# Differential attention by heads instead of by token tiles, with paired score matmuls and the output projection in a written order at the end of its layer

## The chip, the cores and the metric

The kernel runs on one core of a Trainium2 chip. The metric is device time in microseconds (us) of one execution; a profile of one execution, taken by the hardware profiler, stands beside it. The engines are TensorE (PE in the profile, with its weight loads as PEld), VectorE (DVE), ScalarE (ACT), GpSimd (POOL) and SyncE (SP), which issues most of the DMAs.

## The reference, cut to what matters

The program is a two-layer decoder trunk over 512 tokens of width 1024, in float32. Layer 0 runs eight heads of latent attention (MLA) and four heads of differential attention side by side, concatenates their outputs and multiplies them by one matrix; a gated ConvFFN follows. Layer 1 (dilated and stick-breaking attention, then another ConvFFN) is not changed. The part in question:

```python
def diff_attention(q1, q2, k1, k2, v, lam, slopes):          # 4 heads, d = 64, v is 128 wide
    def probs(qb, kf):
        s = einsum('bhqd,bhkd->bhqk', qb, kf) * 64 ** -0.5 - slopes * dist
        return softmax(where(causal, s, -inf))
    p = probs(a1, k1) - lam * probs(a2, k2)
    return einsum('bhqk,bhkd->bhqd', p, v)

o_diff = rms_norm(o_diff, subln_g) * (1.0 - lam_init)        # over the 128 columns of a head
out = concatenate([heads_last(o_mla), heads_last(o_diff)]) @ w_out    # 1024 x 1024
x = x + rms_norm(out, post_g)                                 # sandwich norm, then the FFN's pre-norm
```

## The kernel before, in words

Tokens are handled in four tiles of 128 (NT = 4), taken in the order 3, 2, 1, 0 (`ORDER`), so that the tile with the longest causal row comes first. Activations that feed a projection are kept transposed (columns of the model on the 128 partitions, tokens along the free axis), as two parts, a high and a low one (`xh`, `xl`); so are the weights (`wh` by a ScalarE copy on L71, `wl` by a VectorE subtraction on L72). Each product is three matmuls (`mm3`, L259 to L261). `Weights` streams the matrices in the order of `units`: SP issues a 512 KB load into one of three `wraw` buffers, ScalarE and VectorE split it, and TensorE uses it.

The body of `even` (layer 0) writes, in this order:

- the shared input projections, and `diff_qk(0, z)` for head 0: query (z = 0, into `dq`) and key (z = 1, into `dk`) of a head, 24 matmuls of 512 columns each. The 128 rows of `dq[h]` hold the head's two queries, 64 rows each, and `dk[h]` its two keys;
- MLA: 32 units (head, token tile), each with score, transpose and value steps, staggered by `skewed`. Ten fillers stand behind them in the list: `diff_qk` for heads 1 to 3 (six) and `diff_v` for four token tiles (four, 24 matmuls each). The framework's scheduler places filler instructions where TensorE would wait;
- differential attention: 16 units, token tile by token tile, four heads within a tile. A unit makes two score matmuls, on rows 0 to 63 and 64 to 127 (L787), each into one of the two PSUM banks with the tag "s"; after each, VectorE adds the ALiBi table and takes the minimum on L567, ScalarE exponentiates, and VectorE joins the two on L794. `turn` transposes the difference, `value` multiplies by `dv` (L807), scales, squares on ScalarE, takes the root on GpSimd (`rstd`) and scales by `subg` (L813). After the fourth head of a tile `finish` transposes the tile's four outputs (L821) and splits them into `odh` and `odl`;
- the output projection, `project(i)`, for a token tile: two halves of 512 columns with eight terms of three matmuls each, 48 matmuls. It is the last stage of the last unit of the following tile (`after`), so three of the four tiles run among the units of differential attention, and the last one behind all of them. `chain` then makes the residual, the two norms and the transposed input of the FFN.

The scheduler fixes the order of all engines in layer 0. At the end of layer 1 the order of TensorE, VectorE, ScalarE and GpSimd is written out by hand (`manual_schedule`). The FFN of layer 0 begins with token tiles 3 and 2 and takes the pending transposes of the attention layer among its first matmuls (`pending`).

## Time and profile before

| | |
|---|---|
| median of 3 runs | 1173.12 us (1171.82 to 1174.36) |
| the profiled execution | 1173.26 us, span 1171.4 us |
| TensorE busy in the span | 1151.1 us (98%), weight loads 941.4 us (80%) |
| VectorE, ScalarE, GpSimd busy | 811.3 us, 556.9 us, 56.4 us |
| granted TensorE clock | 0.996 |
| first MLA score / last | 64.0 us / 114.1 us |
| first differential score / last | 159.9 us / 214.8 us |
| first matmul of the FFN (`u`) | 248.7 us |

The span runs from the first to the last instruction. Matmuls are pipelined and their ends are modelled: a matmul of 512 columns in the split form is shown as 0.39 us long, while in a dense run one starts every 0.227 us. So the distance from start to start tells the cost, and the idle time in front of an instruction tells a wait. A float32 matmul that is not a transpose appears as two records. The transposes and score matmuls are in float32; the projections are in the split form.

### The profile page before, as it was taken

Reading aid. Unit: us, or ns where it says so; the run is one execution under the profiler, and the core shown is the slowest. Engines: PE = TensorE matmul, PEld = TensorE weight load, DVE = VectorE, ACT = ScalarE, POOL = GpSimd, SP = SyncE. Lnnn points to the kernel's source line nnn. Section 1 sums busy time; section 2 is a strip of 40 time slices with the busy share of each in tenths; the row PEclk is TensorE's granted clock in tenths of the full one; section 3 lists DMA queues with packets and bytes.
Section 4 is the critical chain, followed back from the end, with each engine's and each line's share of the span. In section 5 each row is a group of like instructions: output and inputs, shape, how many; then the busy total and the mean of one; then the engine's idle time right before and its main releaser. Section 6 shows DMA issues by size and latency. Waiting matters only on the chain. (4 is left out here: it accounts for less than half of the span.)

```text
span 1171.4 us, 15164 instructions
## 1 busy us (share of the span) xinstructions
PE 1151.1 (98%) x5656; PEld 941.4 (80%) x5656; DVE 811.3 (69%) x1424; ACT 556.9 (48%) x942; POOL 56.4 (5%) x138
## 2 busy tenths in 40 slices
PE   8999999999999999999999999999999999999997
PEld 7876766788888888888878877897988888888885
DVE  6677358657666666898973465676676766779896
ACT  5565246445343443456553454544444344345562
POOL 2100002310000000000030000002000000000001
PEclk9999999999999999999999999999999999999999
DMA  7320340033323323345725212222233332324461
GB/s 282 113 81 19 115 126 1 37 129 110 106 90 102 97 90 96 100 146 171 236 100 166 88 55 90 91 74 73 95 124 90 95 103 90 105 84 138 146 202 72
DMA packets 39049, 126.81 MB, mean 108 GB/s; under 512 B 4672, under 2 KB 6336, under 8 KB 38848
## 3 DMA queue, kind: packets, MB, share of 16 engines
q1 hardware_dynamic: 37056, 122.11, 32.6%
q10 hardware_dynamic: 1920, 3.74, 1.0%
q8 instruction: 44, 0.72, 0.3%
q14 instruction: 29, 0.24, 0.1%
HBM read 117.95 MB, written 6.29 MB: 106 GB/s over the span
## 5 line engine op out<-in xcount | busy, mean ns | idle before, releaser
L72 DVE TENSOR_TENSOR wl<-wraw,wh 128x1024 fp32r<-128x1024 f32 (+1 forms) x203 | 245.9, 1219 | 185.4 <-ACT wh L71 184.8
L71 ACT CAST wh<-wraw 128x1024 fp32r<-128x1024 f32 (+1 forms) x203 | 210.6, 1046 | 289.7 <-PE u L260 177.9
L260 PE MATMUL u<-xl,wh 128*128 128x512 f32 (+1 forms) x768 | 285.5, 372 | 0.1
L259 PE MATMUL u<-xh,wh 128*128 128x512 f32 (+1 forms) x768 | 285.1, 372 | 0.2 <-ACT xh L170 0.2
L261 PE MATMUL u<-xh,wl 128*128 128x512 f32 (+1 forms) x768 | 285.3, 372 | 0.0
L261 PEld LDWEIGHTS u<-xh,wl 128*128 128x128 f32 x768 | 144.7, 188 | 25.2
L259 PEld LDWEIGHTS u<-xh,wh 128*128 128x128 f32 x768 | 144.5, 188 | 25.4 <-ACT xh L170 0.6
L260 PEld LDWEIGHTS u<-xl,wh 128*128 128x128 f32 x768 | 144.7, 188 | 25.1 <-DVE xl L171 0.3
L261 PE MATMUL acc<-wh,gl 128*128 128x512 f32 x248 | 96.6, 389 | 0.0
L260 PE MATMUL acc<-wl,gh 128*128 128x512 f32 x248 | 96.6, 389 | 0.0
L259 PE MATMUL acc<-wh,gh 128*128 128x512 f32 x248 | 96.5, 390 | 0.0
L408 ACT ACTIVATE y<-u,cw 128x512 f32<-128x512 f32 x88 | 67.4, 773 | 1.8 <-PE u L261 1.8
L413 ACT ACTIVATE y<-y 128x512 f32<-128x512 f32 x44 | 27.7, 632 | 85.1 <-DVE y L411 85.1
L411 DVE SCALAR_TENSOR_TENSOR y<-u,cw,y 128x510 f32<-128x510 f32 x88 | 65.6, 747 | 2.5
L409 DVE SCALAR_TENSOR_TENSOR y<-u,cw,y 128x511 f32<-128x511 f32 x88 | 65.1, 744 | 0.9 <-ACT y L408 0.9
L177 POOL TENSOR_TENSOR rv<-ms,epst 128x1 f32<-128x1 f32 x40 | 11.2, 282 | 913.2 <-ACT junk L229 842.5
L259 PEld LDWEIGHTS acc<-wh,gh 128*128 128x128 f32 x248 | 46.6, 188 | 10.1 <-issue 0.5
L261 PEld LDWEIGHTS acc<-wh,gl 128*128 128x128 f32 x248 | 46.6, 188 | 9.7
L260 PEld LDWEIGHTS acc<-wl,gh 128*128 128x128 f32 x248 | 46.6, 188 | 9.6
L259 PE MATMUL apt<-xh,wh 128*128 128x512 f32 x128 | 50.7, 396 | 0.0
L260 PE MATMUL apt<-xl,wh 128*128 128x512 f32 x128 | 50.0, 391 | 0.0
L261 PE MATMUL apt<-xh,wl 128*128 128x512 f32 x128 | 49.9, 390 | 0.0
(289 smaller groups left out, 1914.5 us busy)
## 6 DMA issues: line engine op xcount, KB each, us to landing
wraw<-in_ffn_w_up SPq DMA_DIRECT2D x88, 512.0 KB, 3.6
wraw<-in_ffn_w_down SPq DMA_DIRECT2D x44, 512.0 KB, 3.7
wraw<-in_od_w_dqk SPq DMA_DIRECT2D x12, 512.0 KB, 3.7
wraw<-in_ffn_w_down SPq DMA_DIRECT2D x22, 256.0 KB, 2.7
wraw<-in_ev_w_dqk SPq DMA_DIRECT2D x8, 512.0 KB, 3.9
wraw<-in_ev_w_out SPq DMA_DIRECT2D x8, 512.0 KB, 3.8
spill<-X SPq DMA_DIRECT2D x8, 512.0 KB, 2.6
X<-spill SPq DMA_DIRECT2D x8, 512.0 KB, 6.5
```

What stands on the lines that cost most here:

```text
L71: self.nc.scalar.copy(h[:, :w], raw[:, :w])
L72: self.nc.vector.tensor_tensor(l[:, :w], raw[:, :w], h[:, :w].bitcast(F32), ALU.subtract)
L177: POOL.tensor_tensor(v[:, :n], ms, epst[:, :n], ALU.add)
L259: PE.matmul(o, lh, rh, start=first, stop=False, skip_group_check=more)
L260: PE.matmul(o, lh, rl, start=False, stop=False, skip_group_check=more)
L261: PE.matmul(o, ll, rh, start=False, stop=last, skip_group_check=more)
L408: ACT.activation(y[:, z], u, AF.Identity, bias=c[:, 3:4], scale=c[:, 2:3])
L409: DVE.scalar_tensor_tensor(y[:, z, 1:], u[:, :S - 1], c[:, 1:2], y[:, z, 1:], ALU.mult, ALU.add)
L411: DVE.scalar_tensor_tensor(y[:, z, 2:], u[:, :S - 2], c[:, 0:1], y[:, z, 2:], ALU.mult, ALU.add)
L413: ACT.activation(y[:, 0], y[:, 0], AF.Silu)
```

## The change

Only layer 0 is changed.

- The weights of `diff_v` are streamed before those of `diff_qk` for heads 1 to 3, and MLA keeps only the four `diff_v` as fillers.
- Differential attention runs head by head, four token tiles within a head. Its fillers, one every two steps, are `diff_qk` for heads 1 to 3, and then the MLA half (four of the eight terms) of the output projection for token tiles 3 and 2, two halves each.
- A unit takes both PSUM banks before its two score matmuls, which are given high priority and kept next to each other. The first of the two waits until both banks of the unit before are read, and the softmax of the second is made first. The scaling by `subg` is a stage of its own (`norm`). `finish` follows the fourth token tile of a head.
- The query and key of a head share one tile, `dqk{h}`. When heads 0 and 1 are done, their tiles hold the third pair of output weights; those of heads 2 and 3 (`dqk{n}` with n = 2, 3) hold the sums of the last two token tiles.
- The rest of the output projection, 144 of its 192 matmuls, stands behind all units in an order written by hand for four engines, with each tile's norms beside the next tile's matmuls. The last two transposed tiles are handed to the FFN as pending.

The diff, cut to its core:

```diff
+        units += [(A["ev_w_dv"][u], 1024) for u in range(4)]
         for h in range(1, 4):
             units += [(A["ev_w_dqk"][h, z], 1024) for z in range(2)]
-        units += [(A["ev_w_dv"][u], 1024) for u in range(4)]
...
-                    fillers = [lambda h=h, z=z: diff_qk(h, z) for h in range(1, 4) for z in range(2)]
-                    fillers += [lambda i=i: diff_v(i) for i in range(NT)]
                     skewed([[g(p2, i, z) for g in (score, turn, value)]
-                            for p2 in range(4) for i in range(NT) for z in range(2)], fillers, 100)
+                            for p2 in range(4) for i in range(NT) for z in range(2)],
+                           [lambda i=i: diff_v(i) for i in range(NT)], 100)
...
-                wx = es.enter_context(tc.tile_pool(name="ewx", bufs=3, reuse_waits="tile"))
+                wx = es.enter_context(tc.tile_pool(name="ewx", bufs=2, reuse_waits="tile"))
                 W2 = Weights(nc, wx, [(A["ev_w_out"][k], 1024) for k in range(3)], 3, wpool)
-                wout = [W2.next() for _ in range(3)] + [W.next() for _ in range(5)]
+                W2.depth = 1
+                make = W2.pair
+
+                def pair():
+                    if len(W2.made) < 2:
+                        return make()
+                    return [ap.tile([P, D], F32R, tag=f"dqk{n}", name="wo") for n in range(2)]
+
+                W2.pair = pair
+                wout = [W2.next() for _ in range(2)]
...
-                        for z in range(2):
-                            r = slice(z * 64, (z + 1) * 64)
-                            s_ps = bank("s", "sps")
-                            PE.matmul(s_ps[:, :w], dq[h][r, i * P:(i + 1) * P], dk[h][r, :w], start=True, stop=True)
-                            ss.append(softmax_negated(sc, s_ps[:, :w], alibi[:, h, 384 - i * P:], w, 5))
-                        (s1, st1), (s2, st2) = ss
+                        s_ps = [bank("s", "sps") for _ in range(2)]
+
+                        with tc.high_priority():
+                            for z in range(2):
+                                r = slice(z * 64, (z + 1) * 64)
+                                m = PE.matmul(s_ps[z][:, :w], dq[h][r, i * P:(i + 1) * P], dk[h][r, :w],
+                                              start=True, stop=True)
+                                if z:
+                                    tc.keep_in_program_order(m)
+                                else:
+                                    for n in reads:
+                                        tc.add_manual_dep(m.ins, n, SYNC, reason="both banks")
+                        reads.clear()
+                        (s2, st2), (s1, st1) = [softmax_negated(sc, s_ps[z][:, :w], alibi[:, h, 384 - i * P:], w, 5, reads)
+                                                for z in (1, 0)]
...
+                def norm(h, i):
+                    def f(r):
+                        o = otoks[h][:, i]
+                        DVE.scalar_tensor_tensor(o, o, r[:, 0:1], subg[:], ALU.mult, ALU.mult)
+                    return f
...
+                BANK = {3: "aa", 2: "an", 1: "ss", 0: "aa"}
+                accs = {}
+
+                def project(i, half, part):
                     q = slice(i * P, (i + 1) * P)
+                    if i not in accs:
+                        accs[i] = [bank(tag, "ao") for tag in BANK[i]]
+                    o = (oM, oD)[part]
+                    while len(wout) < 4 * part + 4:
+                        wout.append(W.next())
+                    terms = [(o[0][:, k, q], o[1][:, k, q], *wout[4 * part + k]) for k in range(4)]
+                    row_product(accs[i], terms, part == 0, part == 1, (half,))

                 units = []
-                for n, i in enumerate(ORDER):
-                    for h in range(4):
-                        st = [score(i, h), turn(i, h), value(i, h)]
-                        if h == 3:
-                            st.append(finish(i))
-                        if n and h == 3:
-                            st.append(after(n - 1))
+                for h in range(4):
+                    for i in ORDER:
+                        st = [score(h, i), turn(h, i), value(h, i), norm(h, i)]
+                        if i == ORDER[-1]:
+                            st.append(finish(h))
                         units.append(st)
-                skewed(units)
-                after(3)(None)
-                return nx, turns
+                fillers = [lambda h=h, z=z: diff_qk(h, z) for h in range(1, 4) for z in range(2)]
+                last = fillers.pop()
+                fillers.append(lambda: (last(), wout.append(W2.next())))
+                early = [(i, half) for i in (3, 2) for half in range(2)]
+                fillers += [lambda i=i, half=half: project(i, half, 0) for i, half in early]
+                skewed(units, fillers, 2)
+                wout.extend(W.next() for _ in range(4))
...
+                norms, turns = [], []
+                with tc.manual_schedule(engines={PE.engine, DVE.engine, ACT.engine, POOL.engine}):
+                    for n, i in enumerate(ORDER):
+                        t, ms = begin() if n < 2 else (ap.tile([P, D], F32, tag=f"dqk{n}", name="t"), begin_sum())
+                        for half in range(2):
+                            for part in range(2):
+                                if part or (i, half) not in early:
+                                    project(i, half, part)
+                            if half == 0:
+                                part_of(t, ms, 0, accs[i][0], g_post, dve_first=True)
+                                if n > 1:
+                                    turns.pop(0)()
+                                if n:
+                                    j, tj = norms.pop()
+                                    rj = mean_square(X[j][:])
+                        part_of(t, ms, 1, accs[i][1], g_post)
+                        r = rstd(ms[:, 0:1], ms[:, 1:2])
+                        if n:
+                            normed(j, rj, tj)
+                        DVE.scalar_tensor_tensor(X[i][:], t[:], r[:, 0:1], X[i][:], ALU.mult, ALU.add)
+                        norms.append((i, t))
+                        turns.append(turned(i, nx, "to" if n < 2 else "na", t))
+                    r = mean_square(X[i][:])
+
+                def turn_next():
+                    turns[0]()
+                    normed(i, r, t)
+
+                return nx, [turn_next, turns[1]]
```

More of the change, by code (lines that the diff above doesn't have):

```diff
@@ L15 @@
 PSUM = bass.MemoryType.PSUM
+SYNC = mybir.DependencyInfo(mybir.DependencyClass.Sync, mybir.DependencyReason.DATA)
 P = 128
@@ L236, in begin, with begin_sum @@
             return ((pool or chp).tile([P, D], F32, tag=tag, name="t", **({"bufs": 2} if tag in ("z", "sp") else {})),
-                    chp.tile([P, 2], F32, tag="ms", name="ms2", bufs=4))
+                    begin_sum())
+        def begin_sum():
+            return chp.tile([P, 2], F32, tag="ms", name="ms2", bufs=4)
         def residual(i, parts, g, dst=None, at=None):
@@ L549, in even @@
                 ap = es.enter_context(tc.tile_pool(name="ea", bufs=1, reuse_waits="tile"))
-                dq = [ap.tile([P, S], F32, tag=f"dq{h}", name=f"dq{h}") for h in range(4)]
-                dk = [ap.tile([P, S], F32, tag=f"dk{h}", name=f"dk{h}") for h in range(4)]
+                dqk = [ap.tile([P, 2, S], F32, tag=f"dqk{h}", name=f"dqk{h}") for h in range(4)]
+                dq, dk = [t[:, 0] for t in dqk], [t[:, 1] for t in dqk]
                 dv = ap.tile([P, NT, 512], F32, tag="dv", name="dv")
@@ L561, in even, with softmax_negated @@
                 xh, xl = xnT
-                def softmax_negated(sc, ps, table, n, bufs):
+                def softmax_negated(sc, ps, table, n, bufs, reads=None):
                     s = sc.tile([P, S], F32, tag="s", name="s", bufs=bufs)
                     st = sc.tile([P, 2], F32, tag="st", name="st", bufs=6)
-                    DVE.tensor_tensor_reduce(out=s[:, :n], in0=ps, in1=table, scale=1.0, scalar=3e38,
-                                             op0=ALU.add, op1=ALU.min, accum_out=st[:, 0:1])
+                    m = DVE.tensor_tensor_reduce(out=s[:, :n], in0=ps, in1=table, scale=1.0, scalar=3e38,
+                                                 op0=ALU.add, op1=ALU.min, accum_out=st[:, 0:1])
+                    if reads is not None:
+                        reads.append(m.ins.name)
                     ACT.activation(s[:, :n], s[:, :n], AF.Exp, bias=st[:, 0:1], scale=-1.0,
@@ L600, in diff_qk @@
                         if z == 0:
-                            ACT.activation(dq[h][:], acc, AF.Copy, scale=-0.125)
+                            ACT.activation(dq[h], acc, AF.Copy, scale=-0.125)
                         else:
-                            DVE.tensor_copy(dk[h][:], acc)
+                            DVE.tensor_copy(dk[h], acc)
                     with ExitStack() as e2:
@@ L741, in diff_v @@
                             ACT.copy(dv[:, i], a)
-                    fillers = [lambda h=h, z=z: diff_qk(h, z) for h in range(1, 4) for z in range(2)]
-                    fillers += [lambda i=i: diff_v(i) for i in range(NT)]
                     skewed([[g(p2, i, z) for g in (score, turn, value)]
-                            for p2 in range(4) for i in range(NT) for z in range(2)], fillers, 100)
+                            for p2 in range(4) for i in range(NT) for z in range(2)],
+                           [lambda i=i: diff_v(i) for i in range(NT)], 100)
                 sc = es.enter_context(tc.tile_pool(name="esd", bufs=1, reuse_waits="tile"))
+                oD = (sc.tile([P, 4, S], F32R, tag="odh", name="odh"),
+                      sc.tile([P, 4, S], F32R, tag="odl", name="odl"))
                 subg = sc.tile([P, P], F32, tag="subg", name="subg")
@@ L753, in even @@
                 nc.scalar.dma_start(lamb[:], A["ev_lam"].partition_broadcast(P))
+                reads = []
                 neglam = sc.tile([P, 1], F32, tag="neglam", name="neglam")
@@ L773, in even, with score @@
+                def pair():
[4 more added lines that the diff above has]
+                wout = [W2.next() for _ in range(2)]
                 nx = new_xnT()
-                otoks, dens, oDs = {}, {}, {}
-                def score(i, h):
+                otoks, dens = {}, {}
+                def score(h, i):
                     def f(_):
@@ L779, in f @@
                         w = (i + 1) * P
-                        if h == 0:
-                            otoks[i] = sc.tile([P, 4, P], F32, tag="otok", name="otok2", bufs=2)
-                            dens[i] = sc.tile([P, 6, 4], F32, tag="den", name="den", bufs=2)
-                        ss = []
-                        for z in range(2):
-                            r = slice(z * 64, (z + 1) * 64)
-                            s_ps = bank("s", "sps")
-                            PE.matmul(s_ps[:, :w], dq[h][r, i * P:(i + 1) * P], dk[h][r, :w], start=True, stop=True)
-                            ss.append(softmax_negated(sc, s_ps[:, :w], alibi[:, h, 384 - i * P:], w, 5))
@@ L789, in f @@
-                        (s1, st1), (s2, st2) = ss
-                        v = dens[i]
-                        DVE.reciprocal(v[:, 0, h:h + 1], st2[:, 1:2])
-                        DVE.scalar_tensor_tensor(v[:, 1, h:h + 1], v[:, 0, h:h + 1], st1[:, 1:2], neglam[:],
-                                                 ALU.mult, ALU.mult)
-                        DVE.scalar_tensor_tensor(s1[:, :w], s2[:, :w], v[:, 1, h:h + 1], s1[:, :w],
-                                                 ALU.mult, ALU.add)
@@ L796, in f @@
-                        DVE.reciprocal(v[:, 2, h:h + 1], st1[:, 1:2])
-                        return s1
-                    return f
-                def turn(i, h):
-                    return lambda s: transposed(sc, s, i + 1, h % 2, "t")
-                def value(i, h):
+                        if i == ORDER[0]:
+                            otoks[h] = sc.tile([P, NT, P], F32, tag="otok", name="otok2", bufs=2)
+                            dens[h] = sc.tile([P, 6, NT], F32, tag="den", name="den", bufs=2)
@@ new lines, in f @@
+                        reads.clear()
+                        (s2, st2), (s1, st1) = [softmax_negated(sc, s_ps[z][:, :w], alibi[:, h, 384 - i * P:], w, 5, reads)
+                                                for z in (1, 0)]
+                        v = dens[h][:, :, i:i + 1]
+                        DVE.reciprocal(v[:, 0], st2[:, 1:2])
+                        DVE.scalar_tensor_tensor(v[:, 1], v[:, 0], st1[:, 1:2], neglam[:], ALU.mult, ALU.mult)
+                        DVE.scalar_tensor_tensor(s1[:, :w], s2[:, :w], v[:, 1], s1[:, :w], ALU.mult, ALU.add)
@@ L804, in f, with turn, value @@
+                        DVE.reciprocal(v[:, 2], st1[:, 1:2])
+                        return s1
+                    return f
+                def turn(h, i):
+                    return lambda s: transposed(sc, s, i + 1, i % 2, "t")
+                def value(h, i):
                     def f(pt):
@@ L807, in f @@
                             PE.matmul(o[:], pt[:, j], dv[:, j, h * P:(h + 1) * P], start=(j == 0), stop=(j == i))
-                        v, otok = dens[i], otoks[i]
-                        DVE.tensor_scalar(otok[:, h], o[:], v[:, 2, h:h + 1], None, ALU.mult)
+                        v, otok = dens[h][:, :, i:i + 1], otoks[h]
+                        DVE.tensor_scalar(otok[:, i], o[:], v[:, 2], None, ALU.mult)
                         jk = sc.tile([P, P], BF16, tag="jk", name="jk")
-                        ACT.activation(jk[:], otok[:, h], AF.Square, scale=P ** -0.5, accum_out=v[:, 3, h:h + 1])
@@ L812, in f @@
-                        r = rstd(v[:, 3, h:h + 1])
-                        DVE.scalar_tensor_tensor(otok[:, h], otok[:, h], r[:, 0:1], subg[:], ALU.mult, ALU.mult)
-                    return f
-                def finish(i):
-                    def f(_):
-                        otok = otoks[i]
-                        tp = bank("t", "tpo", 4, P)
-                        for j in range(4):
-                            PE.transpose(tp[:, j], otok[:, j], ident[:])
-                        oD = (sc.tile([P, 4, P], F32R, tag="odh", name="odh", bufs=2),
-                              sc.tile([P, 4, P], F32R, tag="odl", name="odl", bufs=2))
-                        split(oD[0][:], oD[1][:], tp[:])
-                        oDs[i] = oD
-                    return f
@@ L828, in project @@
-                def project(i):
-                    oD = oDs.pop(i)
-                    q = slice(i * P, (i + 1) * P)
-                    acc = [bank("a", "ao") for _ in range(2)]
-                    terms = [(oM[0][:, k, q], oM[1][:, k, q], *wout[k]) for k in range(4)]
-                    terms += [(oD[0][:, k], oD[1][:, k], *wout[4 + k]) for k in range(4)]
-                    row_product(acc, terms, True, True, (0,))
-                    if i == ORDER[-1]:
-                        turns.pop(0)()
-                    row_product(acc, terms, True, True, (1,))
-                    return acc
@@ L840, in chain @@
-                def chain(i, acc):
-                    return normalise(i, g_next, nx, "nn", residual(i, acc, g_post))
-                turns = []
-                def after(n):
-                    def f(_):
-                        acc = project(ORDER[n])
-                        if turns:
-                            turns.pop(0)()
-                        turns.append(chain(ORDER[n], acc))
-                    return f
-                units = []
-                for n, i in enumerate(ORDER):
-                    for h in range(4):
-                        st = [score(i, h), turn(i, h), value(i, h)]
-                        if h == 3:
-                            st.append(finish(i))
-                        if n and h == 3:
-                            st.append(after(n - 1))
-                        units.append(st)
@@ L863, in even @@
-                skewed(units)
-                after(3)(None)
-                return nx, turns
+                        ACT.activation(jk[:], otok[:, i], AF.Square, scale=P ** -0.5, accum_out=v[:, 3])
+                        return rstd(v[:, 3])
+                    return f
+                def norm(h, i):
[3 more added lines that the diff above has]
+                    return f
@@ new lines, in finish, with normed @@
+                def finish(h):
+                    def f(_):
+                        tp = bank("t", "tpo", NT, P)
+                        for i in range(NT):
+                            PE.transpose(tp[:, i], otoks[h][:, i], ident[:])
+                        split(oD[0][:, h], oD[1][:, h], tp.rearrange("p a b -> p (a b)"))
+                    return f
+                def normed(i, r, t):
+                    for c in (slice(0, S), slice(S, D)):
+                        DVE.scalar_tensor_tensor(t[:, c], X[i][:, c], r[:, 0:1], g_next[:, c], ALU.mult, ALU.mult)
```

## The prediction

> **What bounds the kernel now.** I read the page first, then windows cut at the stages of layer 0, then TensorE's timeline and waits in the stage that changes. The page:

> ```profile
> span 1171.4 us, 15164 instructions
> ...
> PE 1151.1 (98%) x5656; PEld 941.4 (80%) x5656; DVE 811.3 (69%) x1424; ACT 556.9 (48%) x942; POOL 56.4 (5%) x138
> ```

> TensorE idles for 20.3 us of the span, so the end moves only by what TensorE's own path gains or loses. Two windows (columns: length, PE, PEld, DVE, ACT, POOL busy; clock; DMA share; GB/s): the softmax heads of MLA, then differential attention with three of the four output tiles between its units.

> ```profile
> 63.80:121.80 58.00, 57.97 (x283) 38.24 (x282) 44.46 (x162) 34.61 (x102) 0.00 (x0) 1.00 0.17 52
> 159.90:231.00 71.10, 67.73 (x332) 44.79 (x332) 56.08 (x189) 40.00 (x128) 17.84 (x42) 1.00 0.20 66
> ```

> In the second, TensorE idles 3.4 us and VectorE is busy for 56.1 of 71.1. The clock is 1.00, so no clock is to be won. From 121.8 to 159.9 TensorE runs the leftover projections alone, without a gap. Busy time hides the main cost, which the timeline shows (start, duration, operation, count, wait):

> ```profile
> 161.79 1.74 PE L787 MATMUL sps<-dk,dq 64*128 64x512 f32 x4 [0.78 <-DVE st L567]
> 165.63 0.50 PE L259 MATMUL ao<-wh,omh 128*128 128x512 f32 x1 [0.66 <-ACT wh L71]
> 165.96 0.40 PE L260 MATMUL ao<-wl,omh 128*128 128x512 f32 x1
> 166.29 1.12 PE L787 MATMUL sps<-dk,dq 64*128 64x512 f32 x2
> 167.34 0.49 PE L261 MATMUL ao<-wh,oml 128*128 128x512 f32 x1
> 167.68 0.39 PE L260 MATMUL ao<-wl,omh 128*128 128x512 f32 x1
> ...
> 174.24 1.13 PE L787 MATMUL sps<-dk,dq 64*128 64x512 f32 x4
> 176.53 1.47 PE L787 MATMUL sps<-dk,dq 64*128 64x384 f32 x4
> ...
> 182.18 0.91 PE L787 MATMUL sps<-dk,dq 64*128 64x384 f32 x2
> ```

> One float32 score matmul is two records. At 166.29 a lone one (x2) lasts 1.12 us; at 174.24 two of them, on the two 64-row halves of the array, last 1.13 together. A pair costs what a lone one costs. At 176.53 the second starts when its bank comes free, and the four records take 1.47.

> [...]

> **The change part by part.** The order of the built program (from comparing both programs) has the same number of instructions on every engine. So nothing is removed; order, pairing and waits move.

> *Scores.* A group's path cost is its first start to the next instruction's start: 1.05 us for 512 columns (166.29 to 167.34), 0.84 for 384 (182.18 to 183.02), 0.63 for 256, 0.42 for 128. Around a lone group there is a further 0.20: from 165.96 to 167.68 pass 1.72 us for two projection matmuls (0.227 each by their spacing in runs of their own) and one score, and 1.72 - 0.45 - 1.05 = 0.22. I use 0.20 for each change into and out of the half-array form. Before, by groups of the timeline, waits left out:
> - 512: two pairs, two alone, one staggered at 1.67: 2x1.06 + 2x1.05 + 1.67 = 5.89, five changes;
> - 384: six alone, one staggered at 1.40: 6.44, seven changes;
> - 256: two pairs, two alone, one staggered at 0.89: 3.41, five changes;
> - 128: three pairs, one staggered at 0.63: 1.91, four changes.

> Together 17.65 + 21 x 0.20 = 21.85 us. In the new order 15 of the 16 units have both matmuls next to each other, and one wait covers both banks; the first unit (head 0, last token tile) has three transposes and a projection matmul in between. So 4x(1.06 + 0.84 + 0.63 + 0.42) + 1.05 = 12.85, and 17 x 0.20 = 3.4: 16.25. Saving **5.6 us**, nothing hiding it, since TensorE is the path. If no pair ran together, 32 lone ones would cost 4x2x(1.05 + 0.84 + 0.63 + 0.42) = 23.5 and 6.4, together 29.9: +8.1.

> *Waits of TensorE in this stage:*

> ```profile
> PE sps L787 <- DVE st L567: 1.1, 2, 0.8
> PE tpo L821 <- DVE otok L813: 0.9, 2, 0.6
> PE ao L259 <- ACT wh L71: 0.7, 1, 0.7
> PE tpp L576 <- DVE odl L171: 0.3, 1, 0.3
> PE o L807 <- DVE pt L581: 0.2, 1, 0.2
> ```

> 3.2 us. The first 0.78 and the 0.66 come from the stage's start: the scores stand behind two unread banks, and the only filler is an output projection whose weights ScalarE has not yet split. In the new order head 0's first unit stands inside the end of MLA, with 43 of the 96 matmuls of diff_v after it and then head 1's projections, so I take 1.4 as gone. The 0.9 before the transposes of otok gets a step more of distance (norm is now a stage of its own), but four finishes remain, and the last head has thin cover; there I expect waits of the same size. Bounds: 0 to -3.2. **-1.4.**

> *Fillers.* MLA keeps four diff_v (96 matmuls, 21.8 us) where ten units (240) stood; in its window before it used 73, or 16.6 us, and 41.4 were its own. 96 are more than 73: nothing added. If they ran out, VectorE's 44.5 us for the window less six splits of 1.22 is 37.1, still under the 41.4, so at most short waits like the 0.1 to 0.3 rows. Differential attention now has 144 projection and 48 early output matmuls around it, before 118 output ones. The weights of dqk and the split of W_out are issued in another order on SP's queue, and the FFN's table cw is issued later; the weights land some 3.8 us after issue, and every filler has 5.4 us of matmuls ahead of the next. The split into the old dqk tiles waits for the scores of heads 0 and 1, and what queues behind it on ScalarE and VectorE are softmax steps of head 2; by the order those scores stand a whole head earlier. Nothing for these, 1.2 us (one split) for each that comes late.

> *The dense end.* 144 of 192 output matmuls now run at the end, in a written order, each tile's norm chain beside the next tile's matmuls, two transposes left to the FFN. Layer 1 already ends so, and its waits are the nearest row:

> ```profile
> 811.11 1.23 PE L210 MATMUL tp<-ident,t 128*128 128x128 f32 x8 [0.69 <-DVE t L1188]
> 815.24 0.74 PE L259 MATMUL u<-xh,wh 128*128 128x256 f32 x4 [0.15 <-ACT xh L170]
> ```

> With 0.06 at 816.04 that is 0.9 us. Layer 1's tile has 24 matmuls (5.4 us); here the last two have 48 (10.9), so less would be no surprise. The old end shows no wait from 231.0 to the FFN at 248.7. Bounds 0 and four times 0.9; I take **+0.9**.

> *Sum.* The profiled execution took 1173.26 us, 1.9 of them outside the span; the median of the runs is 1173.12, so 0.1 lower. 1173.26 - 5.6 - 1.4 + 0.9 = **1167.2 us**.

> **The rivals.** *The dense end eats it:* each of the four tiles waits 0.9 (3.6) and the stage's waits come back elsewhere: -5.6 + 3.6 = -2.0, 1171.3 us, within 0.2% (2.3 us, about what a measurement of this kernel can tell from no change). For it: the old end had no such wait. Against it: twice the matmuls cover each chain.

> *Both banks at once (slower):* a pair starts only when VectorE has read both banks of the unit before. Its two reads and their accumulator reads took 1.3 us (161.04 to 162.35), and TensorE stood 0.78 at 161.79 with nothing in between. If all 16 pairs met that, 12.5 us come back: 1167.2 + 12.5 = 1179.7. It decides where the work between two pairs is shorter than VectorE's reads. In the new order that is at least three projection matmuls with six small ones (0.68 + 0.66 = 1.34 us) and mostly six to nine; break-even is half the price at every pair. [...]

> *The pairs do not run together:* 8.1 + 5.6 instead of the saving: 1167.2 + 13.7 = 1180.9. The pairs at 174.24 and 191.21 speak against it.

> **How the numbers follow.** Forecast 0.82, dense end 0.10 (same), both banks 0.06, no concurrency 0.02 (slower). The range: at best all 3.2 us of waits go and the end adds none, 1173.26 - 5.6 - 3.2 = 1164.5; at worst the dense end's 1171.3. That leaves out 0.08 and some error at the ends.

> **What would show it.** Right: score groups x4 of about 1.13, 0.91, 0.70 and 0.49, only the first two alone; the FFN's first u matmul at about 242.6 instead of 248.7, and no difference growing after it. Wrong: a wait of sps on VectorE's st summing to several us; waits of tp on t beyond 0.9 us in the last 33 us before the FFN; idle TensorE between 64 and 122 us; groups of x4 lasting over 2 us.

## The result: 4.35 us less in the profiled executions, 0.44% in the runs

The changed kernel takes 1168.91 us in the median of five runs (1166.98 to 1169.09), the kernel before 1173.26 in five (1171.82 to 1174.36): ratio 0.9956, 95% interval 0.9945 to 0.9967. In two further sets of runs (e5 and e9 below) the ratio was 0.9953 [0.9938, 0.9968] and 0.9943 [0.9922, 0.9964]. So it is faster by a little, clear of the interval, and 1.7 us above the forecast of 1167.2.

Two lines of the changed kernel's page; the profiled execution took 1168.91 us, its span is 4.3 us shorter:

```profile
span 1167.1 us, 15181 instructions
...
PE 1145.5 (98%) x5656; PEld 939.4 (80%) x5656; DVE 810.8 (69%) x1424; ACT 558.2 (48%) x942; POOL 57.4 (5%) x138
```

Windows over MLA, differential attention and the dense end (columns as in the prediction):

```profile
63.70:121.80 58.10, 58.01 (x278) 37.39 (x277) 41.59 (x160) 31.68 (x97) 0.00 (x0) 1.00 0.11 34
112.50:206.80 94.30, 90.76 (x463) 65.08 (x463) 63.53 (x206) 48.17 (x134) 13.90 (x32) 1.00 0.27 87
206.80:241.40 34.60, 34.60 (x164) 28.80 (x163) 15.80 (x21) 13.13 (x28) 5.67 (x16) 1.00 0.11 46
```

MLA still has cover (0.1 us idle), and the dense end has no gap at all. The attention in the middle idles 3.5 us, as much as before. Its pairs, in TensorE's timeline, one head's four and one that waits:

```profile
147.04 1.13 PE L805 MATMUL sps<-dqk 64*128 64x512 f32 x4
150.44 0.92 PE L805 MATMUL sps<-dqk 64*128 64x384 f32 x4
153.10 0.70 PE L805 MATMUL sps<-dqk 64*128 64x256 f32 x4
155.32 0.49 PE L805 MATMUL sps<-dqk 64*128 64x128 f32 x4
...
169.75 0.92 PE L805 MATMUL sps<-dqk 64*128 64x384 f32 x4 [0.77 <-DVE st L571]
```

All 15 pairs start together, and the rows last what the forecast gave them. The waits of TensorE from 63 to 262 us, all that the view names:

```profile
PE tpp L582 <- DVE s L818: 1.6, 1, 1.6
PE sps L805 <- DVE st L571: 0.8, 1, 0.8
PE tpp L582 <- DVE odl L172: 0.6, 1, 0.6
PE o L830 <- DVE otok L832: 0.4, 2, 0.2
```

The sum is 3.4 us where it was 3.2. The names have changed, the total has not.

Where the time went can be followed by matching the two traces. The best point is the start of layer 1 (first `apt`), which both kernels reach in the same way: 624.50 us before, 618.38 after, 6.12 less. The first `u` (248.95 and 241.38) shows more, because the pending transposes fall at another place among the `u`. The lead of 6.1 to 6.2 us is there once the FFN's first half has run, and stays through layer 0's FFN. But the last matmul is only 4.34 us earlier (1162.82 and 1158.48). The missing 1.8 us are lost behind that point, 1.5 of them inside the attention of layer 1, which the change does not touch. Windows cut at the steps of the granted clock show it:

```profile
653.34:656.75 3.41, 2.46 (x12) 1.82 (x11) 3.41 (x8) 1.12 (x1) 0.00 (x0) 1.00 0.75 180
656.75:660.16 3.41, 3.41 (x9) 2.63 (x9) 2.03 (x5) 2.08 (x2) 0.00 (x0) 0.50 0.35 132
```

For 3.41 us the clock is 0.50, and 9 matmuls are started in it, where the next 3.41 us, at 1.00, have 16. In front of it stand the last scores of the stick-breaking attention with a wait in them:

```profile
655.38 0.92 PE L1011 MATMUL zp<-sq,sk 64*128 64x256 f32 x4 [0.82 <-DVE z L1015]
```

In the profile of before the same scores, with the same wait of 0.82 us, were followed by no half clock; what differs is measured under e5.

### The profile page after: what moved, and what is told of

It is laid out like the page before. It is cut to its first block, busy times and chain, and to the rows that moved or that the text cites. A ratio compares the mean times of both kernels' runs of the same rounds, so it can differ in the third digit from the quotient of the medians.

```text
span 1167.1 us, 15181 instructions
## 1 busy us (share of the span) xinstructions
PE 1145.5 (98%) x5656; PEld 939.4 (80%) x5656; DVE 810.8 (69%) x1424; ACT 558.2 (48%) x942; POOL 57.4 (5%) x138
## 5 line engine op out<-in xcount | busy, mean ns | idle before, releaser
L73 DVE TENSOR_TENSOR wl<-wraw,wh 128x1024 fp32r<-128x1024 f32 (+1 forms) x202 | 244.5, 1218 | 186.2 <-ACT wh L72 185.8
L263 PEld LDWEIGHTS acc<-wh,gh 128*128 128x128 f32 x248 | 46.5, 188 | 10.2 <-issue 0.5
```

Source lines behind the costliest of these rows:

```text
L73: self.nc.vector.tensor_tensor(l[:, :w], raw[:, :w], h[:, :w].bitcast(F32), ALU.subtract)
L263: PE.matmul(o, lh, rh, start=first, stop=False, skip_group_check=more)
```

## The experiments

Two questions were put to the chip: what makes the 6 us, and why 1.8 are lost again. The measure for the first is the start of layer 1, which the second does not reach. "Groups" are the unbroken runs of half-height score matmuls in TensorE's record; their cost is the distance from the first start to the next instruction's start, less the wait. "Waits" are all idle time of TensorE from 63 to 262 us. A half-clock window is a stretch at granted clock 0.50; the column counts those between the start of the program and layer 1, without the first one that most traces have (11.63 to 15.04 us in the changed kernel, 12.89 to 16.30 before). Each row is one profiled execution.

| kernel | groups | cost of groups | waits | half clock before layer 1 | layer 1 starts |
|---|---|---|---|---|---|
| before | 20 | 17.8 | 3.4 | none | 624.5 |
| changed | 17 | 12.9 | 3.7 | none | 618.4 |
| request undone (e1) | 18 | 14.1 | 3.5 | none | 619.0 |
| pairs alone in before (e2) | 17 | 12.9 | 7.8 | none | 626.1 |
| lone scores (e3) | 32 | 23.5 | 0.9 | none | 628.0 |
| projections back in MLA (e4) | 17 | 13.0 | 6.8 | 10.2 us | 625.6 |
| no early output products (e8) | 17 | 12.9 | 7.7 | 6.8 us | 626.4 |
| one token tile early (e12) | 17 | 12.9 | 6.8 | 6.8 us | 624.7 |
| e3 and e4 together (e11) | 29 | 26.5 | 8.2 | 20.5 us | 643.4 |

Layer 0 is the same program in the changed kernel and in e5, e6, e9 and e10. There layer 1 starts at 618.2 to 619.0 us, so rows that lie 0.8 us apart are not told apart.

### Pairs: the request, the pairs alone, and no pairs

**e1_unasked** writes the scores as before, in the new order of heads and fillers:

```diff
-  s_ps = [bank("s", "sps") for _ in range(2)]
-  with tc.high_priority(): ...      # both matmuls, manual dependency, fixed order
-  (s2, st2), (s1, st1) = [softmax_negated(...) for z in (1, 0)]
+  for z in range(2):
+      s_ps = bank("s", "sps")
+      PE.matmul(s_ps[:, :w], dq[h][r, ...], dk[h][r, :w], start=True, stop=True)
+      ss.append(softmax_negated(...))
```

> The changed kernel with the scores written as before the change: no wait for both banks, no priority, no fixed order, softmax of z=0 first. In the built order of TensorE 14 of the pairs still stand together, with 4 lone scores (18 groups; the changed kernel has 15 pairs and 2 lone, 17 groups). Theory A (what counts is how many groups of half-height matmuls TensorE enters, and the work beside them decides that): one group more, at 0.4 to 1.06 us a group: the feed-forward part's first u product at 241.8 to 242.5 us, 1169.3 to 1170.0 us in all. Rival B (the request itself, both banks first with priority, brings the 5.6 us): the first u product at 246 to 247 us, 1174 us. A half-clock window in layer 1, or none, moves a whole time by 1.6 us either way, so the start of the feed-forward part is the better measure.

Measured: layer 1 at 619.0 us, 1167.75 us in all (1167.25 to 1170.3), ratio to before 0.9955 [0.9938, 0.9973], where the changed kernel has 0.9956. Rival B falls. Theory A holds in kind, but its figures were a little dear: the first `u` came at 240.9 us and the whole time lies 1.6 us below the least that it gave. With other work to choose from, the scheduler left 14 of 16 units paired without being asked, and no run shows a gain from asking.

**e2_pairs_only** is the other half: the kernel before with the request for pairs, and nothing else of the change.

> The kernel before with the pairing alone: both score banks first, priority, fixed order, softmax of z=1 first; token tiles in their old order, projections of the heads 1 to 3 still beside the first attention, output projection still tile by tile. Built order: 17 groups (15 pairs, 2 lone) as in the changed kernel, against 20 runs of records before. Theory A (the groups alone are the gain): the first u product about 5 us earlier than the 248.9 us of before, at 243.5 to 244.5, 1167.5 to 1168.5 us. Rival C (pairs need other work beside them: without the head projections as fillers TensorE waits for the score banks and the softmax as long as it saves): the first u product at 248 to 249.5 us, 1172 to 1174 us.

Measured: 1174.14 us (1172.61 to 1175.23), ratio 1.0005 [0.9996, 1.0014]; layer 1 at 626.1. The groups are as cheap as in the changed kernel, 4.9 us less than before, and the waits take 4.4 us of it. Layer 1 starts 1.6 us later than before all the same, because the other matmuls cost some 2 us more in this trace, 1.1 of it at the projections. Four of the seven rows of its waits:

```profile
PE o L819 <- DVE otok L821: 1.8, 4, 0.6
PE sps L792 <- DVE st L568: 1.5, 5, 0.6
PE tpp L579 <- DVE pt L584: 1.2, 1, 1.2
...
PE tpp L579 <- DVE s L806: 0.9, 2, 0.5
```

Each is a step of the softmax or value chain of a unit, all behind VectorE; the waits for the score banks themselves are 1.5 us of the 7.8. A reading that would fit is that lone scores filled such time before, and that pairs leave it empty unless a projection stands there. That agrees with rival C (its figures were passed by 0.3 us at the first `u`), but it is argued and not shown: which edit of e2 (the two banks, the priority, the order of the softmax) brings each wait was not taken apart.

**e3_singles** makes every score of the changed kernel wait until the bank of the score ahead is read (`add_manual_dep` on each score instead of each pair, no priority), so that no pair is left.

> The changed kernel with every score made to stand alone: the score of one z waits until VectorE has read the bank of the score ahead of it, so that 32 lone groups run instead of 15 pairs and 2 lone (17 groups). All else as in the changed kernel. Theory A: a lone score costs what a pair of its width costs (1.06, 0.85, 0.63, 0.42 us for 512, 384, 256, 128 columns by the changed kernel's rows), so 32 of them cost 4 x 2 x 2.96 = 23.7 us instead of 12.9: +10.8 us; the first u product at 252 us, 1179.7 us in all. Rival D (the records' distances overstate what a group costs on the path, and the gain came from the order of heads and the dense end): less than +4 us, below 1173 us.

Measured: 1176.43 us (1175.29 to 1178.61), ratio to before 1.0024 [1.0014, 1.0034]; layer 1 at 628.0, 9.6 us later than with pairs. The groups cost 10.6 us more, as worked out; the longer scores cover the waits (3.7 to 0.9, so 2.8 back), and the other rows cost 1.8 us more (value products 1.0, projections and output 1.6, less 0.8 elsewhere). Theory A holds for the groups. The whole time is 3.3 us below what it gave, 1.2 of it at the start of layer 1; the profile of e3 also has no half-clock window in layer 1. One of its rows, to be read beside the paired one of the changed kernel above:

```profile
148.95 1.12 PE L804 MATMUL sps<-dqk 64*128 64x512 f32 x2
```

One score of 512 columns (x2) lasts 1.12 us, two (x4) lasted 1.13. By start to next start the pair takes 1.06 us (147.04 to 148.10) and the lone score 1.05 (148.95 to 150.00).

### Cover: what stands beside the pairs

**e4_qk_in_mla** puts the projections of heads 1 to 3 back beside the first attention; pairs, order of heads and dense end stay (the weights are loaded in the order of before again):

```diff
-  skewed([... p2, i, z ...], [lambda i=i: diff_v(i) for i in range(NT)], 100)
+  skewed([... p2, i, z ...], [lambda ...: diff_qk(h, z) for h in range(1, 4) for z in range(2)]
+         + [lambda i=i: diff_v(i) for i in range(NT)], 100)
...
-  fillers = [lambda ...: diff_qk(h, z) for h in range(1, 4) for z in range(2)]
+  fillers = [lambda: None] * 5 + [lambda: wout.append(W2.next())]
```

> The changed kernel with the projections of the heads 1 to 3 put back beside the first attention, as before the change (their weights loaded ahead of those of the values again); pairs, head order, early output products and dense end stay. Built order: 17 groups, 15 pairs. Theory A (groups alone): the same as the changed kernel within 1 us, the first u product at 241 to 242.5 us, 1168 to 1170 us. Rival C (pairs need other work beside them): waits of TensorE for the score banks and the transposes' inputs of 5 to 8 us more in the attention by pairs; the first u product at 246 to 250 us, 1174 to 1177 us.

Measured: 1174.8 us (1173.66 to 1178.52), ratio 1.0018 [1.0007, 1.003]; layer 1 at 625.6, so 7.2 us later with the same 17 groups. Only 3.1 of it are waits, fewer than the 5 to 8 that rival C gave. The rest follows them. Windows of 3.41 us at the last head, cut at the clock's steps:

```profile
205.23:208.64 3.41, 1.96 (x10) 1.05 (x9) 1.76 (x5) 0.99 (x3) 1.26 (x3) 1.00 0.00 0
208.64:212.05 3.41, 1.10 (x6) 0.83 (x5) 0.70 (x2) 0.40 (x2) 0.74 (x2) 0.50 0.00 0
212.05:215.47 3.42, 2.75 (x8) 1.82 (x8) 1.34 (x2) 0.59 (x1) 0.00 (x0) 0.50 0.00 0
215.47:218.88 3.41, 3.41 (x10) 2.63 (x9) 0.05 (x1) 0.69 (x2) 0.19 (x1) 0.50 0.00 0
```

TensorE is starved while the last units go through their softmax (1.96, then 1.10 us busy of 3.41), the clock goes to 0.50 from 208.64 to 218.88 us, and the dense output products in that stretch start further apart:

```profile
214.16 0.63 PE L265 MATMUL ao<-wh,odl 128*128 128x512 f32 x1
214.59 0.63 PE L263 MATMUL ao<-wh,odh 128*128 128x512 f32 x1
```

From start to start that is 0.43 us, and 0.22 to 0.24 at 219.10 to 219.79 us, when the clock is 1.00 again. The 192 output products cost 51.0 us instead of 45.3, so 5.7 us more, which is more than the waits; 3.2 come back at `diff_v`, which stands alone again. So the price that rival C gave held, mostly by the half clock, which no theory had named.

**e8_no_early** and **e12_one_tile_early** change only the amount of cover at the last head: `early` empty, or `(3, half)` alone, instead of the two tiles 3 and 2.

> The changed kernel without the four early half products of the output (48 of its 192 matmuls): all of the output projection is dense at the end, and the last head's softmax has 48 matmuls less beside it. Theory C (pairs need other work beside them): waits of TensorE of 3 to 6 us more in the last third of the attention by pairs, perhaps a half-clock window after them; layer 1 starts at 621 to 626 us instead of 618.4. Theory A (only the number of groups counts): layer 1 starts at 618 to 619 us.

> The changed kernel with the early half products of one token tile (24 matmuls of the output projection) beside the last head instead of two (48). With two, layer 1 starts at 618.4 to 618.9 us; with none, at 626.4, of which 3.5 us are waits at the last head and 4 us a half-clock stretch of 6.8 us right after. Theory C with W (what lacks is cover for the last head's softmax, and a long enough gap then halves the clock): 1.5 to 3 us of waits more than with two, layer 1 at 620 to 622 us where no half-clock window follows and 623 to 625 where one or two do. Rival (one tile is enough cover): 618.4 to 619.2 us.

Measured: 1175.82 us (ratio 1.0023 [1.0014, 1.0032]) and 1174.84 us (1.0008 [0.9995, 1.0021]); layer 1 at 626.4 and 624.7. Without 48 early products the changed kernel is slower than the one before; with half of them it gains nothing. Theory C, with the half clock in e12, holds for both; each came out just past the dearer end in one figure (layer 1 at 626.4 in e8, 3.1 us of waits more in e12). The whole time of e12 also has a half-clock window in layer 1. The wait that matters is the same row, of 2.31 us, in both and in e4, here from the timeline of e8, with the window around it and the next:

```profile
204.81 1.09 PE L848 MATMUL tpo<-ident,otok 128*128 128x128 f32 x4 [2.31 <-DVE otok L841]
```

```profile
201.02:204.44 3.42, 0.71 (x3) 0.30 (x2) 1.04 (x4) 0.40 (x2) 1.08 (x3) 1.00 0.00 0
204.44:207.85 3.41, 2.37 (x7) 1.77 (x8) 0.91 (x2) 0.59 (x1) 0.00 (x0) 0.50 0.03 5
```

It is the end of the last head's chain: value, norm, then the transposes of `otok`. By the timelines of e4, e8 and e12, TensorE is already inside the first tile's `odh` products by then and has done those of heads 0 to 2; what comes next in the written order needs head 3, and the products of the other tiles that need nothing of it stand behind, out of reach. In the changed kernel 23 matmuls of `omh` and `oml`, emitted early and free to move, fill the stretch from 199.8 us to the last transposes at 206.5.

**e11_singles_in_mla** undoes both, pairs (as in e3) and cover (as in e4).

> The changed kernel with both undone: the head projections of heads 1 to 3 back beside the first attention, and each score made to wait until the bank of the one ahead is read. Built order: 29 groups, 26 of them lone, so groups cost about 8.7 us more than with 17. Layer 1 starts at 618.4 us in the changed kernel, 628.0 with lone scores alone, 625.6 with the projections moved back alone. Theory C (the pairs pay only where other work stands beside them, so without it they gain little): layer 1 at 627 to 631 us. Rival (the two add up): 635 us; more than that, up to 638, if lone scores wait too where nothing else is to be done.

Measured: 1191.44 us (1190.83 to 1201.19), ratio 1.0163 [1.0127, 1.0199]; layer 1 at 643.4, beyond every figure expected. Theory C in its strong form (pairs pay little without cover) falls: from e11 to e4 the pairs are worth 17.8 us, from e3 to the changed kernel 9.6. About 20.5 us at half clock, against 10.2 in e4, are part of it; they raise the groups' own cost to 26.5 us. What e2 shows is therefore narrower: against a kernel that already had 11 of its 16 units in pairs (four of them staggered), pairs alone gain nothing.

### The wait at 137 us

The longest wait, 1.62 us for the first unit, stood behind VectorE's splits of the output weights, which waited for ScalarE, which waited for DMAs. VectorE's timeline of the changed kernel, then ScalarE's:

```profile
132.01 1.23 DVE L73 TENSOR_TENSOR wl<-wraw,wh 128x1024 fp32r<-128x1024 f32 x1 [1.15 <-ACT wh L72]
...
135.14 1.23 DVE L73 TENSOR_TENSOR wl<-wraw,wh 128x1024 fp32r<-128x1024 f32 x1 [1.24 <-ACT wh L72]
136.28 0.75 DVE L818 SCALAR_TENSOR_TENSOR s<-s,den 128x512 f32<-128x512 f32 x1
```

```profile
130.93 1.04 ACT L72 CAST wh<-wraw 128x1024 fp32r<-128x1024 f32 x1 [0.99 <-DMA wraw<-in_ev_w_out]
...
134.06 1.05 ACT L72 CAST wh<-wraw 128x1024 fp32r<-128x1024 f32 x1 [1.36 <-DMA wraw<-in_ev_w_out]
```

**e7_wout_later** asks for the three blocks one by one, with the last three head projections (`wout = []`, and `W2.next()` in each of those fillers).

> The changed kernel with the first three blocks of the output weights asked for later, one with each of the last three head projections, instead of two ahead of the attention by pairs. Theory V (the 1.62 us wait at 137.2 us comes from splits of those two blocks that stand in VectorE's queue ahead of the softmax and wait for DMAs that have not landed): that wait is gone or below 0.3 us, the start of layer 1 at 616.7 to 617.2 us instead of 618.4, about 1167.3 us in all with the window of half clock, 1165.7 without. Rival (VectorE is full there, another instruction takes the place): a wait of 1 us or more stays in the first third of the attention by pairs, layer 1 starts at 618.0 to 618.8 us.

Measured: 1168.82 us (1167.29 to 1169.55), layer 1 at 618.7. The 1.62 row is gone, as theory V said, but the time is not won (V gave 616.7 to 617.2). The rival's figure for layer 1 holds; no single wait reaches its 1 us, but four of one kind come to 2.8:

```profile
PE sps L805 <- DVE st L571: 2.8, 4, 0.9
```

The pairs now wait for VectorE's reads of the banks (0.8 us in the profile of the changed kernel, 1.7 in that of e5). By VectorE's timeline the splits stand elsewhere, two of them from 129.32 us right ahead of the read that the longest of these waits ends with.

### The half-clock window in layer 1

**e5_changed_again** is the changed kernel itself.

> The changed kernel once more, for where its half-clock window falls. [...] Rival (the change itself slows layer 1): the window is there each time.

Measured: 1168.08 us (1166.99 to 1168.9). Layer 1 starts at 618.9, the span is 1166.0 and no half-clock window follows the `zp` scores, with the same wait of 0.82 us. The clock's steps give each trace a grid: in the trace of the changed kernel the first two spells at 0.50 are recorded as 3.413 us long each, the first ends at 15.04 us, the second at 660.16, 189 such lengths later, and a last one begins at 1161.92, behind the last matmul, another 147 later. On e5's grid the window that held the scores, and the next:

```profile
653.06:656.47 3.41, 2.46 (x13) 1.35 (x10) 3.23 (x6) 1.94 (x2) 0.00 (x0) 1.00 0.57 161
656.47:659.88 3.41, 3.41 (x17) 2.75 (x16) 2.86 (x7) 1.25 (x2) 0.00 (x0) 1.00 0.48 151
```

TensorE was busy for the same 2.46 us as in the window that was followed by half clock. By the timelines, though, this one starts 0.8 us earlier in the work and holds two steps of 384-column `zp`, in which both halves of the array run at once (in the trace of the changed kernel the two matmuls of such a step start within 0.01 us of each other, at 652.70 and at 653.03); the other holds only lone half-height ones, the wait and the first 0.5 us of `apt`. The other profiles bear this out. In twelve (all but e6 and e10) these scores have the same two waits, and what differs is where they fall on the grid of the trace's own clock steps. They start 1.60, 1.66 and 1.82 us after a step in e12, e7 and the changed kernel, and there the half clock follows; in the other nine they start 0.77 to 1.33 or 2.65 to 3.27 us after one, and none follows. The kernel before is among the nine, at 3.27. So in these profiles the phase separates the two cases, and the change does not, nor does busy time alone. What in the work ahead of a step sets the clock behind it is not shown.

**e6_zp_covered** takes the waits away: two of the four `apv` tiles are emitted between the three parts of the first `zp` scores.

```diff
-  for i in ORDER:
+  for i in ORDER[:2]:
       tile_V(i)
...
   for n, (j0, o0, o1) in enumerate(spans):
+      if cover and n:
+          tile_V(cover[n - 1])
       zp = [bank(t, "zp") for t in ("ss", "nt", "ss")[n]]
```

> The changed kernel with two of the four apv tiles of layer 1 (the projection of the values) emitted between the three parts of the first zp scores, so that TensorE has full-array products where it waited 0.82 and 0.13 us. Nothing else is changed. [...]

Theory W in the next two texts is the author's conjecture that the half clock comes with the waits among these scores, in some executions and not in others, by how the waits fall against the clock's steps.

> The changed kernel, beside the next one on the same chip. Theory W: whole times between 1167.0 and 1169.0 us, the upper ones with a half-clock window in layer 1 after the zp scores, the lower ones without.

> The changed kernel with two apv tiles between the first zp scores (as in the earlier run), beside the changed kernel on the same chip. Theory W: the 0.9 us of waits gone in every execution and the half-clock window near 657 us in none: 1.5 to 2.0 us less than the changed kernel in the median, 1166.2 us. Rival (the window comes elsewhere instead): 1167.2 us or more, no different from the changed kernel by over 0.1%.

Measured: 1166.11 us (1165.65 to 1168.36) against 1168.08 for the changed kernel on one chip, 1166.19 (1165.74 to 1167.04) against 1167.62 (1166.53 to 1169.22) on another; ratios to before 0.9941 [0.9926, 0.9956] and 0.9929 [0.9911, 0.9948]. From layer 1's first `apt` matmul to its last pass 132.1 us in the changed kernel with the window, 130.6 without (e5, e9), 129.2 with the cover (e6, e10). So 1.4 us come from the waits and the forms around them, more than the 0.9 of the waits, and a further 1.5 in executions that would have had the window. Neither covered profile has the window. Of the fifteen times of the changed kernel (its own, e5 and e9) eight are above 1168 us, of the ten covered ones one. So theory W holds in the main for what it gave of e9 and e10, and this version is faster than both kernels. What W gave too well: the 1.43 us between the medians of e9 and e10 are a little under its 1.5 to 2.0, and one covered time (1168.36, in e6, whose times spread by 2.7 us) is as long as those with a window. That one was not profiled, so what slowed it is open.

## Why the prediction was right

*Scores, -5.6.* Right in kind and nearly in size. The prediction's groups without switches came to 17.65 us before and 12.85 after; measured 17.78 and 12.89, so -4.9. The further 0.8 for four switches less is not separable in the trace. The assumed 0.20 us a switch is probably too much: in e3 15 groups more cost the other rows 1.8 us, so 0.12 a group by estimate. Scores that did not run together were priced at 13.7 over the new order, 10.65 of it for the groups; by e3 against the changed kernel it was 10.6 for the groups and 9.6 in sum, since the longer scores cover 2.8 us of waits.

*Waits, -1.4.* Wrong. The wait at the start of the stage did go, but others came: 3.4 us again. The step that failed is the one that called the first unit safe because work stood after it on TensorE. VectorE ran splits of weights that had not landed ahead of the first unit's softmax, and that cost 1.62 us.

*Fillers, nothing.* The net was near nothing, but the reasoning hid a term. One late split was priced at 1.2 us; it was 1.6 (1.2 to 1.9 in the other profiles of this order). What was not priced is what the fillers are worth beside the pairs: 7.2 us for the six head projections (e4) and 8.0 for the four early half products of the output (e8), the half clock included. The saving on scores was booked to the pairs alone. In the kernel before, pairs alone save nothing (e2).

*The dense end, +0.9.* Too high: no wait in 34.6 us. The 192 output matmuls cost 45.3 us instead of 49.7, since they no longer stand among transposes and scores; the 96 of `diff_v`, which now do, cost 25.0 instead of 21.9. So the mixing moved, and 1.3 us of it are won, a term that the sum did not have. The value products gain another 1.1 and the transposes of the scores lose 0.8. With 4.9 for the groups and 0.3 more of waits that makes 6.2, against the 6.12 at the start of layer 1.

*"The clock is 1.00, so no clock is to be won"* and *no difference growing after the FFN's start*: true for layer 0 of this kernel, wrong for the span. In the profiled execution 1.8 us are lost between layer 1's start and the end, of which the half-clock window is the main part. With no window the changed kernel's profiled executions took 1167.1 (e9) and 1167.8 (e5), at the forecast and 5.4 to 6.1 us below the profile of before, which has none either. How near the forecast came is in part luck: the scores were 0.7 too good and the waits 1.7, the end 0.9 too bad, and the 1.6 us that mixing, values and transposes gained were not in the sum.

*The rivals.* "Both banks at once" did not decide in the changed kernel (0.8 us of such waits, 0.6 to 1.7 in other profiles of it), where projection matmuls stand between most pairs. In e2 waits do eat the gain, but only 1.5 of the 7.8 us are for the banks. "The dense end eats it" and "the pairs do not run together" are excluded by the rows above.

## What to carry to other kernels

A score matmul on half the array's rows cost as much alone as with its partner here (1.05 and 1.06 us at 512 columns), so count the groups; but see that enough independent work stands between the pairs, and that some of it is left, and not queued behind what waits, for the chain at the very end. A gap of TensorE cost its own length and, where the dense work behind it ran at clock 0.50, more than as much again (in e4 3.1 us of waits and 5.7 at the output products): look at the granted clock after each gap, not only at the gap. When a wait ends with another engine, ask what stands ahead in that engine's order, and whether its data have landed.
